# Joints of a streaming-encoder layer: chunk 2's operands copied inside SBUF, sums and splits reordered, a third raw weight buffer in the gates

## The chip, the core and the metric

One core of a Trainium2 chip runs the whole kernel. The time is the device time of one execution in microseconds (us); the figure given for a kernel is the median of its runs. A profile is one execution taken by the hardware profiler. Engines: TensorE (PE, its weight loads PEld), VectorE (DVE), ScalarE (ACT), GpSimd (POOL) and SyncE (SP), which here issues nearly all DMAs, in order.

## The reference

One layer of a chunk-causal encoder over 1024 prompt tokens and 32 sample tokens that share the weights; D = 1024, hidden size of the MLP 4096, fp32 throughout:

```python
h = rms_norm(x, g_mix)
q, k, v, ch, cb, cc, ga, gb = split(h @ w_in)
a = window_attention(q, k, v, sink) @ w_attn_out
u = cc * ch
bo = (cb * causal_conv3(u)) @ w_conv_out
x = x + (sigmoid(ga) * a + sigmoid(gb) * bo) @ w_mix_out
hc = rms_norm(x, g_cross)
x = x + cross_attention(hc @ w_cq, mem_k, mem_v) @ w_co
hm = rms_norm(x, g_mlp)
x = x + square(relu(hm @ w_up)) @ w_down
y = rms_norm(x, g_final)
```

The outputs are y of both groups, and the new keys, values, convolution rows and memory keys and values.

## The kernel before

**Number format.** TensorE works on fp32r operands. Each fp32 operand is split in two: a high half (ACT casts it, L127) and a low half (DVE subtracts the high one, L128; for activations `split_here`, L1255 to L1258). Each product is three matmuls into one accumulator: wh·hi, wh·lo, wl·hi.

**Layout.** Activations lie with features on the 128 partitions (NF = 8 tiles of features) and tokens along the free axis. Up to the cross-attention the 1056 tokens go in chunks of 384, 384 and 288 (`CH`). The last chunk holds the sample. In the MLP they go in two halves of 528 (HT), each of two quarters of 264 (QT).

**Stages, in order of time.**
- Norm, input projection, convolution and window attention (0 to some 550 us), then the attention output.
- The gates. `gate_pair(f)`, f = 1 to 7, computes two column tiles of the gate weights at once with seven half products in place of eight, in Winograd's form. For that it needs sums of weight quarters. POOL makes them earlier: `sum_step` loads a piece (tile `ws` or the shared tile `xacc`), makes four adds and stores it (gsum_d; for the down projection wsum_d).
- Three trunks, one per chunk: eight tiles of w_conv_out and eight of w_mix (`do_mix`) as fillers. `beside` runs one step of the cross-attention of the chunk before after each filler: row statistics (`chunk_stats`), `do_cq`, head units (`scores`, `turn`, `values`) and `do_co`, which adds w_co's product to the residual x1 and has `square_acc` add the squares on POOL.
- `normed(c, f)` (L1243) multiplies x1 by gain and row factor into a temporary (tag "ct", a ring of six) and stores it to DRAM (xn_d, by token halves). For chunk 0 it also splits it in SBUF.
- Up projection of token half 0, w_up's first 16 of 32 tiles paired with the others by `UP`: six weights per quarter in two passes (`up_one`, q = 0 and q = 1, 24 matmuls of 264 columns each), then ten weights for both quarters at once (`up_two`, two items of 24 each). Beside these 32 fillers the cross-attention of chunk 2 and the norm of chunks 1 and 2 are done.
- The sums joint. `comb_load` loads both token halves from xn_d, `comb_sums(k)` makes four combined operands (n3, t2, n1, n4) and splits all four; `up_fetch` and `up_sums` load raw weights and have POOL make their sums; `up_start` begins.
- The paired stage, `up_pair(i)`, i = 0 to 15: the rest of the up projection in the same form, over weight and token halves. It stores hidden activations and their sums to DRAM (op_d, called b_d, n_d and t_d in the rows), which are the operands of the down projection.
- Down projection: stages b11, b21, n4, t2, n3, n1, b22 (`stage`, eight items each by output tile pair j and half t of the 16 operands). After each item `pump2(2)` splits the operands loaded last and loads two of the next stage. Then `final` writes y, chunk by chunk.

**What sets the order.** A planner places the program's operations on the engines; `pin` keeps an instruction at its place in program order. Buffers come from pools of fixed depth. SP's queue is in order, so a DMA that waits for a buffer holds up all that follow it. Weights come through `fetch_w` (raw, tag "wr", two buffers), `issue_w` (split into "wh" and "wl", three buffers each) and `next_w`, which keeps two weights ready beyond the one in use (LOOK = 2). For a weight in `kept` the low half is stored to DRAM (wl_d) at its first use, and loaded at later ones in place of DVE's subtraction.

The accumulators of the stages up to the sums are three buffers (tag "acc"). `lslot` gives one of six tiles of 528 columns (tag "lt"). `put` collects stores, and `flush` issues them at the next item. L854 to L856 are the three matmuls of `product` (gates and up projection), L1640 to L1642 those of the down projection, L216 the column sums of the row statistics, L1310 `up_two`'s copy of an accumulator.

Of the kernel before, what the change touches and what calls it, by code (L numbers as in the profile page):

```python
# [40 lines left out]
def hybrid_step(ctx: ExitStack, tc: tile.TileContext, io):  # L41
# [46 lines left out]

    gsum_d = dram.tile([7, P, 2, 2, 512], F32, name="gsum_d")
# [52 lines left out]
    fetched = []  # L142

    def fetch_w():
        raw = wp.tile([P, 1024], F32, tag="wr", bufs=2, name=nm("wr"))
        src = weight(worder[wpos[0] + len(fetched)])
        sp.dma_start(raw.rearrange("p (i c) -> p i c", i=4) if len(src.shape) == 3 else raw, src)
        fetched.append(raw)
# [536 lines left out]
    pieces += [(j, t, i) for j in range(4) for t in range(2) for i in range(4)]  # L685

# [6 lines left out]
    def sum_step():  # L693
        old = W.pop("new", None)
        if pieces:
            at = pieces.pop(0)
            t = sum_tile(len(pieces))
            if at[0] == "g":
                _, f, q = at
                for e in range(2):  # L700
                    src = io["w_in"][34 + 8 * e + f].rearrange("p (h c) -> p h c", h=2)
                    pin(pool_e.dma_start(t[:, 2 * e : 2 * e + 2], src[:, :, 256 * q : 256 * q + 256]))
            else:
                pin(pool_e.dma_start(t, io["w_down"][at]))
            W["new"] = at, t
        if old:
# [3 lines left out]
            if at[0] == "g":  # L710
                _, f, q = at
                for w in range(2):
                    pin(pool_e.dma_start(gsum_d[f - 1][:, w, :, 256 * q : 256 * q + 256], t[:, 2 * w : 2 * w + 2]))
            else:
                pin(pool_e.dma_start(wsum_d[at], t))
# [152 lines left out]
    def close_gates():  # L868
        pump(0)
        assert not wanted  # L870
        closed(Y["cm"])
        open_top()
        for c in (1, 2):
            wanted.extend((bcp[c], k, bc_d[c][:, k], CH[c][1], lambda c=c: yslot(c)) for k in range(NF))
# [21 lines left out]
    def gate_pair(f):  # L896
# [22 lines left out]
        w1 = take(("w_in", 34 + f))  # L919
        load_a(0)  # L920
# [6 lines left out]
        fetch_w()  # L927
# [71 lines left out]
    def after_gates():  # L999
# [5 lines left out]
        m_cm, mpool = opened("mpool", bufs=16, reuse_waits="tile")  # L1005
# [168 lines left out]
    def do_co(c, half):  # L1174
        def fn(w):
# [3 lines left out]
            for f in fs:  # L1179
# [9 lines left out]
                square_acc(x, f, c)  # L1189
# [14 lines left out]
    def close_cross():  # L1204
        closed(cr_cm)

    def open_sums():
        closed(Y["cm"])
        closed(Y["cm", 1])
        S["s"] = ctx.enter_context(tc.tile_pool(name="sums", bufs=8, reuse_waits="tile"))  # L1210
        L["cm"], L["pool"] = opened("late", bufs=1, reuse_waits="tile")

# [30 lines left out]
    def normed(c, f):  # L1243
        t = tmp(CH[c][1])
        pin(dve.scalar_tensor_tensor(t, x1[c][f], col(G_MLP + f), R[c], op0=ALU.mult, op1=ALU.mult))
        for h, to, at in in_halves(c):
            sp.dma_start(xn_d[h][:, f, to], t[:, at])
# [31 lines left out]
    UP = [(8 * g + i, 8 * g + i + 4) for g in range(4) for i in range(4)]  # L1279

    def up_one(i, q):


        def fn(w):
# [9 lines left out]
            act.activation(h, h, AF.Relu)  # L1294
            pool_e.tensor_tensor(h, h, h, op=ALU.mult)
# [4 lines left out]
    def up_two(i):  # L1300
# [14 lines left out]
        def second():  # L1315
# [6 lines left out]
            pool_e.tensor_tensor(h, h, h, op=ALU.mult)  # L1322
# [7 lines left out]
    def comb_load(kinds):  # L1330
        for kind in kinds:
            for k in range(4):
                h, f = {"t2": (0, k), "n1": (1, k), "n3": (1, k + 4), "n4": (0, k + 4), "b22": (1, k + 4)}[kind]
                pool = S["b" if kind == "b22" else "s"]
                hi, lo = comb[kind, k] = tuple(slot(pool, kind, HT) for _ in range(2))
                sp.dma_start(lo.bitcast(F32), xn_d[h][:, f])

    def raw(kind, k):
        return comb[kind, k][1].bitcast(F32)

    def comb_sums(k):
        both = xacc_tile()
        n3, n1 = both[:, :HT], both[:, HT:]
        t2, n4 = lslot(), lslot()
        pin(dve.tensor_sub(n3, raw("n1", k), raw("n3", k)))
        pin(dve.tensor_sub(t2, raw("t2", k), n3))
        pin(dve.tensor_sub(n1, raw("t2", k), raw("n1", k)))
        pin(pool_e.tensor_tensor(n4, raw("n4", k), t2, op=ALU.subtract))
        for kind, x in (("t2", t2), ("n1", n1), ("n3", n3), ("n4", n4)):
            hi, lo = comb[kind, k]  # L1350
            pin(act.copy(hi, x))
            pin(dve.tensor_sub(lo, x, hi.bitcast(F32)))
# [7 lines left out]
    raws, wset = {}, {}  # L1360

# [56 lines left out]
    def up_pair(i):  # L1418
# [10 lines left out]
        doubled(banks_of(B[i]), wset[i, 3], 0, "n3", False)  # L1429
        h22 = lt()  # L1430
# [21 lines left out]
        m3, m2 = lt(), lt()  # L1452
        dve.tensor_sub(m3, h12, h22)
        put(op_d["n3"][:, i], m3)
        dve.tensor_sub(m2, h11, m3)
        put(op_d["t2"][:, i], m2)
        pool_e.tensor_tensor(h12, h11, h12, op=ALU.subtract)
        put(op_d["n1"][:, i], h12)
# [11 lines left out]
        m4 = h11  # L1470
        pool_e.tensor_tensor(m4, h21, m2, op=ALU.subtract)
        put(op_d["n4"][:, i], m4)
# [40 lines left out]
    def cross_steps(c):  # L1513
        units = [Cross(c, h) for h in ([0, 1, 2, 3] if c < 2 else [4, 0, 1, 2, 3])]
        nu = len(units)
        steps = [("call", [mem_load] if c == 0 else [mem_load_s] if c == 1 else [])]
        steps.append(("call", [lambda: chunk_stats(c)]))
        steps.append(("items", [(do_cq(c, j), ("w_cq", j)) for j in range(2)]))
        for i in range(nu + 2):
# [7 lines left out]
            steps.append(("call", calls))  # L1527
            if i < nu:
                steps.append(("call", []))
        if c == 2:  # L1530
            steps.append(("call", [close_cross]))
        steps.append(("items", [(do_co(c, 0), ("w_co", 0))]))
        steps.append(("items", [(do_co(c, 1), ("w_co", 1))]))
        steps.append(("call", [lambda: chunk_stats(c)]))
# [24 lines left out]
    left = beside([], trunk(0), [(i, lambda: pump(2)) for i in range(NF)])  # L1559
    item(lambda: pump(0))  # L1560
    left = beside(cross_steps(0), trunk(1))
# [8 lines left out]
    late = [(f // 2, lambda f=f: normed(1, f)) for f in range(NF)]  # L1570
    late += [(3 + f // 4, lambda f=f: second_load(f)) for f in range(NF)]
    late += [(4 + f // 4, lambda f=f: second_split(f)) for f in range(NF)]
    steps = left + cross_steps(2)
    at = len(steps)
    late.append((at, open_sums))
    late += [(at + f // 4, lambda f=f: normed(2, f)) for f in range(NF)]
    late.append((at + 1, lambda: comb_load(["t2", "n4"])))
    late.append((at + 2, lambda: comb_load(["n3", "n1"])))
    late += [(at + 4 + 2 * k, lambda k=k: comb_sums(k)) for k in range(4)]
    late.append((at + 4, lambda: up_fetch(0)))  # L1580
    late.append((at + 7, lambda: up_sums(0)))
    late.append((at + 9, lambda: up_fetch(1)))
    assert at + 11 <= len(fillers)
    left = beside(steps, fillers, late)
    assert not left
    worder.append(STOP)

    def up_start():
# [3 lines left out]
        comb_load(["b22"])  # L1592
        up_issue(0, 3)
        up_sums(1)
        up_t2(0)
        comb_split("b22")
# [47 lines left out]
    def banks_for(j, q):  # L1644
        if q is None:
            return banks_of(wide_tile())
        if j % 2 == 0:
            bank["pair"] = wide_tile()
        one = bank["pair"][:, j % 2, :QT]
        return [one, None] if q == 0 else [None, one]  # L1650

    def prod(kind, j, t, then, q=None):


        def fn(w):
            if t == 0:
                bank[j] = banks_for(j, q)
# [198 lines left out]
```

## Time and profile before

| | |
|---|---|
| median of 3 runs | 1796.79 us (1793.31 to 1799.98) |
| the profiled execution | 1801.2 us, span 1799.4 us |
| mean granted clock of TensorE | 0.984 |
| PE busy | 1743.8 us, 97% of the span |
| DVE, ACT, POOL busy | 66%, 47%, 33% |
| DMA | 346.79 MB, mean 193 GB/s; HBM 251.97 MB read, 92.68 MB written |
| share of 16 DMA engines | hardware queue q1 49.8%, software queue q0 7.8% |
| chain that ended last | PE 85%, DMA 6%, DVE 4% |

The span is that of the instructions; the profiled time has 1.8 us more around it. A row of a group reads: line, engine, operation, output<-inputs by the program's names, shape, count, then busy time and mean ns of one, then the idle time before it and what ended most of that. A row of waits reads: the waiting engine and group, the group that released it, the idle time in us, how often, and the longest one. A row of the timeline reads: start, duration, and in brackets the idle time before and its releaser. SPq is SP issuing a DMA.

### The profile page before, as it was taken

Reading aid. Unit: us, or ns where it says so; the run is one execution under the profiler, and the core shown is the slowest. Engines: PE = TensorE matmul, PEld = TensorE weight load, DVE = VectorE, ACT = ScalarE, POOL = GpSimd, SP = SyncE. Lnnn points to the kernel's source line nnn. Section 1 sums busy time; section 2 is a strip of 40 time slices with the busy share of each in tenths; the row PEclk is TensorE's granted clock in tenths of the full one; section 3 lists DMA queues with packets and bytes.
Section 4 is the critical chain, followed back from the end, with each engine's and each line's share of the span. In section 5 each row is a group of like instructions: output and inputs, shape, how many; then the busy total and the mean of one; then the engine's idle time right before and its main releaser. Section 6 shows DMA issues by size and latency. Waiting matters only on the chain.

```text
span 1799.4 us, 32416 instructions
## 1 busy us (share of the span) xinstructions
PE 1743.8 (97%) x12214; PEld 1722.0 (96%) x12214; DVE 1185.3 (66%) x2215; ACT 851.1 (47%) x1648; POOL 596.9 (33%) x659
## 2 busy tenths in 40 slices
PE   8999999999999999999999989979999999999997
PEld 8999999999999999998999988979999999999997
DVE  7776767868666747446675867686666676556664
ACT  8643535435344334334565756554444443433443
POOL 0013245653453444402224241445565400000021
PEclk9999999999999999999999989989999999999999
DMA  5332234344347887868756767565676675555554
GB/s 182 110 101 92 87 113 145 122 147 142 127 151 245 300 291 258 281 205 267 258 198 199 236 222 225 202 232 185 224 230 220 219 262 175 188 181 185 181 177 144
DMA packets 181084, 346.79 MB, mean 193 GB/s; under 512 B 18480, under 2 KB 101712, under 8 KB 180800
## 3 DMA queue, kind: packets, MB, share of 16 engines
q1 hardware_dynamic: 167152, 296.32, 49.8%
q0 software_dynamic: 13776, 48.41, 7.8%
q8 instruction: 96, 1.57, 0.4%
q14 instruction: 60, 0.49, 0.1%
HBM read 251.97 MB, written 92.68 MB: 192 GB/s over the span
## 4 chain that ended last, share of the span: by engine, by line
PE 85%; DMA 6%; DVE 4%; issue 2%; ACT 1%; SPq 1%; POOL 0%; DVEq 0%; ACTq 0%; POOLq 0%
PE acc L185 12%; PE acc L187 12%; PE acc L186 12%; PE acc L1640 6%; PE acc L1642 6%; PE acc L1641 6%; PE acc L854 5%; PE acc L856 5%; PE acc L855 5%; PE pc L856 2%; PE pc L855 2%; PE pc L854 2%; PE pt L574 2%; DVE wl L128 1%; DMA wr<-in_w_up 1%
## 5 line engine op out<-in xcount | busy, mean ns | idle before, releaser
L127 ACT CAST wh<-wr 128x1024 fp32r<-128x1024 f32 x223 | 234.1, 1050 | 440.6 <-PE acc L1641 142.0
L128 DVE TENSOR_TENSOR wl<-wr,wh 128x1024 fp32r<-128x1024 f32 x223 | 287.9, 1291 | 144.3 <-ACT wh L127 143.3
L185 PE MATMUL acc<-X,wh 128*128 128x384 f32 (+1 forms) x864 | 282.1, 327 | 7.0 <-ACT wh L127 7.0
L186 PE MATMUL acc<-X,wh 128*128 128x384 f32 (+1 forms) x864 | 279.3, 323 | 0.0
L187 PE MATMUL acc<-X,wl 128*128 128x384 f32 (+1 forms) x864 | 278.7, 323 | 0.3 <-DVE wl L128 0.3
L261 POOL TENSOR_TENSOR xacc<-xacc,ct 128x384 f32<-128x384 f32 (+1 forms) x62 | 79.9, 1293 | 332.9 <-ACT ct L259 331.0
L185 PEld LDWEIGHTS acc<-X,wh 128*128 128x128 f32 x864 | 163.1, 189 | 7.6 <-ACT wh L127 7.0
L186 PEld LDWEIGHTS acc<-X,wh 128*128 128x128 f32 x864 | 163.4, 189 | 0.6
L187 PEld LDWEIGHTS acc<-X,wl 128*128 128x128 f32 x864 | 163.1, 189 | 0.9 <-DVE wl L128 0.8
L185 PE MATMUL acc<-Y,wh 128*128 128x384 f32 (+1 forms) x432 | 138.8, 323 | 0.7 <-ACT Y L764 0.7
L186 PE MATMUL acc<-Y,wh 128*128 128x384 f32 (+1 forms) x432 | 139.3, 323 | 0.1
L187 PE MATMUL acc<-Y,wl 128*128 128x384 f32 (+1 forms) x432 | 139.3, 323 | 0.0
L1641 PE MATMUL acc<-n,wh 128*128 128x264 f32 x352 | 101.9, 289 | 2.2 <-DVE n L1258 2.2
L1640 PE MATMUL acc<-n,wh 128*128 128x264 f32 x352 | 101.4, 288 | 0.0
L1642 PE MATMUL acc<-n,wl 128*128 128x264 f32 x352 | 101.2, 288 | 0.0
L127 ACT CAST PTh<-pt 128x512 fp32r<-128x512 f32 (+3 forms) x94 | 45.8, 517 | 109.5 <-PE pt L574 108.7
L709 POOL TENSOR_TENSOR ws<-ws 128x256 f32<-128x256 f32 x92 | 81.6, 887 | 7.1 <-DMA ws<-in_w_down 1.9
L709 POOL TENSOR_TENSOR xacc<-xacc 128x256 f32<-128x256 f32 x92 | 82.1, 892 | 4.9
L185 PEld LDWEIGHTS acc<-Y,wh 128*128 128x128 f32 x432 | 80.9, 188 | 1.1 <-ACT Y L764 1.1
L186 PEld LDWEIGHTS acc<-Y,wh 128*128 128x128 f32 x432 | 81.1, 188 | 0.4 <-DVE Y L765 0.4
L187 PEld LDWEIGHTS acc<-Y,wl 128*128 128x128 f32 x432 | 81.1, 188 | 0.0
L560 ACT ACTIVATE S<-S,nmx 128x257 f32<-128x257 f32 (+1 forms) x132 | 64.2, 488 | 18.7 <-DVE nmx L555 17.3
(398 smaller groups left out, 5557.8 us busy)
## 6 DMA issues: line engine op xcount, KB each, us to landing
wr<-in_w_up SPq DMA_DIRECT2D x54, 512.0 KB, 4.2
wr<-in_w_in SPq DMA_DIRECT2D x53, 512.0 KB, 3.8
wr<-wsum_d SPq DMA_DIRECT2D x40, 512.0 KB, 3.6
wr<-in_w_conv_out SPq DMA_DIRECT2D x24, 512.0 KB, 4.3
wr<-in_w_mix SPq DMA_DIRECT2D x24, 512.0 KB, 4.3
wr<-in_w_down SPq DMA_DIRECT2D x24, 512.0 KB, 3.7
wl<-wl_d SPq DMA_DIRECT2D x20, 512.0 KB, 4.1
n_d<-Z SPq DMA_DIRECT2D x32, 264.0 KB, 4.5
```

The costliest lines, as they stand in the source:

```text
L127: act.copy(hi, src)
L128: dve.tensor_sub(lo, src, hi.bitcast(F32))
L185: pe.matmul(out, wh[:, a], hi, start=(k == 0), stop=False)
L186: pe.matmul(out, wh[:, a], lo, start=False, stop=False)
L187: pe.matmul(out, wl[:, a], hi, start=False, stop=(k == len(acts) - 1))
L709: pin(pool_e.tensor_tensor(t[:, to], t[:, x], t[:, y], op=ALU.add))
L854: pe.matmul(acc, wh[:, a], hi, start=(start and k == 0), stop=False, skip_group_check=True)
L855: pe.matmul(acc, wh[:, a], lo, start=False, stop=False, skip_group_check=True)
L856: pe.matmul(acc, wl[:, a], hi, start=False, stop=(k == 3), skip_group_check=True)
L1640: pe.matmul(a, wh[:, s], hi, start=(t == 0 and k == 0), stop=False, skip_group_check=True)
L1641: pe.matmul(a, wh[:, s], lo, start=False, stop=False, skip_group_check=True)
L1642: pe.matmul(a, wl[:, s], hi, start=False, stop=(t == 1 and k == 7), skip_group_check=True)
```

## The change

1. Gates: a third raw weight buffer (`wr3`), taken in turn by every third fetch from f = 1 to f = 7, with one fetch more at the start and none in the last pair.
2. `sum_step` gets four more pieces, the weight sums of the first two up pairs (usum_d). `up_ready` loads them, so `up_sums` is no longer called for pairs 0 and 1; `up_second` loads the one raw weight that is needed.
3. The mix pool has 18 buffers instead of 16, and the first conv output of chunk 1 stands between the conv outputs and the mix of chunk 0. The operand pool of chunk 1 is reopened above the others in `close_gates`.
4. `normed` of chunk 0 runs from filler 2 of the third trunk, formerly from 6. The cross-attention of chunk 2, the norms and the sums are put between the 32 up fillers by a table, `then(i, …)`, in place of `beside`'s one step per filler. Column and row part of the statistics stand apart there.
5. `do_co` for c > 0, f > 4 keeps squares as tiles of their own; the column sum on PE takes them one by one.
6. The low halves of the six weights of `up_one` are `kept`. Squared ReLU: one DVE instruction in `up_one`; in `up_two` ACT squares after its ReLU. POOL's multiplication goes in both.
7. `open_sums` comes before `do_co` of chunk 2 and loads the tokens of chunks 0 and 1 from xn_d into the operand buffers (16 DMAs). `normed` of chunk 2 copies its tile from SBUF into the buffers of n1 and n3, beside the store of features 4 to 7. `comb_sums` uses a single sums tile, casts and splits t2 alone, and returns n3, n1 and n4 raw into their buffers by DMA; they are split in `comb_split` later, b22 and n4 inside `up_pair(0)`.
8. The last pair's sums n3, t2, n1, n4 are made within stage b11, after item (1, 0). Stage b11 goes through two output tiles per half t (`paired`). Each j gets an accumulator of its own in the last stage too. `pump2(3)` in place of `pump2(2)`.

```diff
     def fetch_w():
-        raw = wp.tile([P, 1024], F32, tag="wr", bufs=2, name=nm("wr"))
+        if third:
+            third["n"] += 1
+        if third and third["n"] % 3 == 0:
+            raw = third["pool"].tile([P, 1024], F32, tag="wr3", name=nm("wr3"))
+        else:
+            raw = wp.tile([P, 1024], F32, tag="wr", bufs=2, name=nm("wr"))
...
+    pieces += [("u", i, q) for i in range(2) for q in range(2)]
...
         w1 = take(("w_in", 34 + f))
+        if f == 1:
+            third.update(n=2, pool=Y["top"])
+            fetch_w()
+        if f == NF - 1:
+            third.clear()
...
-        fetch_w()
+        if f < NF - 1:
+            fetch_w()
...
-                square_acc(x, f, c)
+                if c and f > 4:
+                    sq = tmp(n)
+                    act.activation(sq, x, AF.Square)
+                    accs[c].append(sq)
+                else:
+                    square_acc(x, f, c)
...
+        for kind in ("t2", "n1", "n3", "n4"):
+            for k in range(4):
+                comb[kind, k] = tuple(slot(S["s"], kind, HT) for _ in range(2))
+        n = CH[1][0] + CH[1][1] - HT
+        for k in range(4):
+            sp.dma_start(raw("t2", k), xn_d[0][:, k])
+            sp.dma_start(raw("n1", k)[:, :n], xn_d[1][:, k, :n])
+            sp.dma_start(raw("n3", k)[:, :n], xn_d[1][:, k + 4, :n])
+            sp.dma_start(raw("n4", k), xn_d[0][:, k + 4])
...
-            sp.dma_start(xn_d[h][:, f, to], t[:, at])
+            if c < 2 or f > 3:
+                sp.dma_start(xn_d[h][:, f, to], t[:, at])
+        if c == 2:
+            sp.dma_start(raw("n1" if f < 4 else "n3", f % 4)[:, HT - CH[c][1] :], t)
...
-            act.activation(h, h, AF.Relu)
-            pool_e.tensor_tensor(h, h, h, op=ALU.mult)
+            dve.scalar_tensor_tensor(h, h, 0.0, h, op0=ALU.max, op1=ALU.mult)
...
-        both = xacc_tile()
-        n3, n1 = both[:, :HT], both[:, HT:]
-        t2, n4 = lslot(), lslot()
+        n3, n1 = xacc[0][:, :HT], xacc[0][:, HT:]
+        t2 = L["pool"].tile([P, 1024], F32, tag="wr2", bufs=2, name=nm("t2"))[:, :HT]
         pin(dve.tensor_sub(n3, raw("n1", k), raw("n3", k)))
+        sp.dma_start(raw("n3", k), n3)
         pin(dve.tensor_sub(t2, raw("t2", k), n3))
         pin(dve.tensor_sub(n1, raw("t2", k), raw("n1", k)))
-        pin(pool_e.tensor_tensor(n4, raw("n4", k), t2, op=ALU.subtract))
-        for kind, x in (("t2", t2), ("n1", n1), ("n3", n3), ("n4", n4)):
-            hi, lo = comb[kind, k]
-            pin(act.copy(hi, x))
-            pin(dve.tensor_sub(lo, x, hi.bitcast(F32)))
+        sp.dma_start(raw("n1", k), n1)
+        hi, lo = comb["t2", k]
+        pin(act.copy(hi, t2))
+        pin(dve.tensor_sub(lo, t2, hi.bitcast(F32)))
+        pin(pool_e.tensor_tensor(t2, raw("n4", k), t2, op=ALU.subtract))
+        sp.dma_start(raw("n4", k), t2)
...
+        if i == 0:
+            comb_split("b22")
+            comb_split("n4")
...
+        if last:
+            behind.append(lambda: [more(sums()), flush()])
+        else:
+            more(m2)
...
+    trunks = [trunk(c) for c in range(3)]
+    trunks[0].insert(NF, trunks[1].pop(0))
...
-    left = beside(left + cross_steps(1), trunk(2), normeds(0, 6))
+    left = beside(left + cross_steps(1), trunks[2], normeds(0, 2))
...
+    kept.update((("w_up", UP[i][0]), None) for i in range(NQ))
...
+    then(16, call(open_sums))
+    then(17, lambda: item(do_co(2, 0), ("w_co", 0)))
+    then(18, lambda: item(do_co(2, 1), ("w_co", 1)))
+    then(19, call(open_late), call(chunk_col, 2))
+    then(20, call(chunk_row, 2))
+    then(21, call(xacc_tile))
+    for f in (0, 4, 1, 5, 2, 6, 3, 7):
+        then(21, call(normed, 2, f))
+    for k in range(4):
+        then(23 + k, call(comb_sums, k))
+    then(27, call(up_second, 0))
+    then(28, call(comb_split, "n1"))
...
-        if j % 2 == 0:
-            bank["pair"] = wide_tile()
-        one = bank["pair"][:, j % 2, :QT]
-        return [one, None] if q == 0 else [None, one]
+        banks = banks_of(wide_tile())
+        return banks if q is None else [banks[0], None] if q == 0 else [None, banks[1]]
...
+    paired = [(j + i, t) for j in (0, 2) for t in range(2) for i in range(2)]
...
-        for n, (j, t) in enumerate(steps):
+        for n, (j, t) in enumerate(paired if kind == "b11" else steps):
             def fn(ws, j=j, t=t):
                 prod(kind, j, t, then, q)(ws)
-                pump2(2)
+                pump2(3)
+                if behind and (j, t) == (1, 0):
+                    behind.pop()()
```

More of the change, by code (lines that the diff above doesn't have):

```diff
@@ L86, in hybrid_step @@
     wsum_d = dram.tile([4, 2, 4, P, 4, 256], F32, name="wsum_d")
+    UP = [(8 * g + i, 8 * g + i + 4) for g in range(4) for i in range(4)]
+    usum_d = dram.tile([2, P, 2, 2, 512], F32, name="usum_d")
     gsum_d = dram.tile([7, P, 2, 2, 512], F32, name="gsum_d")
@@ L871, in close_gates @@
         closed(Y["cm"])
+        closed(Y["cm", 1])
         open_top()
+        Y["cm", 1], Y[1] = opened("ypool1", bufs=16, reuse_waits="tile", side="right")
         for c in (1, 2):
```

149 lines of the change are left out of this document (86 added, 63 removed).

## The prediction

> **What bounds the kernel now.** I read the page first, then the busy time by stretches, then who made TensorE wait, then the chain of waits and the timeline around each of those places.
>
> ```profile
> span 1799.4 us, 32416 instructions
> PE 1743.8 (97%) x12214; PEld 1722.0 (96%) x12214; DVE 1185.3 (66%) x2215; ACT 851.1 (47%) x1648; POOL 596.9 (33%) x659
> ```
>
> TensorE is busy 97% of the span, and the changed program gives it the same matmuls, but for 18 of one column. So only what is lost beside that work can be won. The stretches show it: window, busy time (and count) of PE, PEld, DVE, ACT, POOL, then granted clock, DMA share and GB/s.
>
> ```profile
> 600.00:675.00 75.00, 75.00 (x472) 74.99 (x471) 41.89 (x59) 24.04 (x47) 34.04 (x42) 1.00 0.86 290
> 675.00:700.00 25.00, 22.07 (x119) 20.98 (x118) 18.02 (x26) 11.84 (x20) 12.02 (x14) 0.93 0.81 267
> 825.00:875.00 50.00, 46.61 (x262) 45.02 (x261) 33.96 (x53) 26.82 (x47) 10.68 (x9) 1.00 0.79 269
> 1025.00:1060.00 35.00, 29.82 (x170) 27.32 (x169) 26.11 (x42) 17.38 (x33) 18.17 (x17) 0.85 0.65 220
> 1040.00:1125.00 85.00, 77.15 (x540) 75.18 (x541) 58.80 (x113) 50.95 (x117) 27.20 (x27) 0.90 0.69 219
> 1060.00:1120.00 60.00, 52.87 (x387) 51.22 (x387) 40.43 (x79) 36.65 (x83) 12.53 (x14) 0.91 0.73 225
> 1160.00:1225.00 65.00, 51.24 (x365) 49.18 (x364) 50.88 (x55) 28.12 (x52) 31.02 (x21) 0.89 0.58 200
> 1225.00:1430.00 205.00, 205.00 (x1684) 205.00 (x1683) 134.53 (x168) 94.20 (x127) 116.02 (x80) 1.00 0.68 220
> 1430.00:1480.00 50.00, 47.78 (x362) 46.85 (x362) 39.36 (x68) 28.13 (x45) 5.98 (x4) 0.93 0.74 260
> 1725.00:1750.00 25.00, 22.69 (x158) 21.77 (x157) 14.90 (x23) 9.88 (x15) 5.02 (x4) 0.86 0.39 128
> ```
>
> A stall costs twice: the idle time, and then matmuls at half clock, which the mean clock shows. Loss of a stretch = (window − PE busy) + (1 − clock) × window:
> - 675:700, gates: 2.9 + 1.8 = 4.7 us
> - 825:875, first mix: 3.4 + 0 = 3.4
> - 1025:1060, end of the third trunk: 5.2 + 5.2 = 10.4
> - 1060:1120, up projection of the first quarters: 7.1 + 5.4 = 12.5
> - 1160:1225, sums before the paired stage: 13.8 + 7.2 = 20.9
> - 1430:1480, up to down: 2.2 + 3.5 = 5.7
> - 1725:1750, before the last product: 2.3 + 3.5 = 5.8
>
> Together 63.4 us: the ceiling of this change. The paired stage (1225:1430) loses nothing; it gives a 264-column matmul as 205 / 1684 = 0.122 us.
>
> ```profile
> PE acc L854 <- ACT lt L1310: 10.1, 3, 5.6
> PE acc L854 <- ACT wh L127: 5.9, 4, 2.6
> PE pr L233 <- ACT ct L231: 3.4, 1, 3.4
> PE acc L1184 <- DVE Gb L1046: 2.7, 4, 1.1
> PE acc L1641 <- DVE n L1258: 2.2, 2, 1.3
> PE acc L1641 <- DVE b L1258: 1.7, 2, 1.1
> ```
>
> **The change, part by part.**
>
> Gates. The raw weight waits for its buffer, not for the link: DVE splits it late behind 16 operand splits, only then SP can load.
>
> ```profile
> 677.27 1.21 DVE L128 TENSOR_TENSOR wl<-wr,wh 128x1024 fp32r<-128x1024 f32 x1
> 678.51 0.32 SPq L147 DMA_DIRECT2D wr<-gsum_d  x1
> 685.25 1.04 ACT L127 CAST wh<-wr 128x1024 fp32r<-128x1024 f32 x1 [3.69 <-DMA wr<-gsum_d]
> ```
>
> A third raw buffer lets that load go one weight earlier, some 6 us, more than the 3.69 that ACT idled. I leave 0.5 us: gain 4.2 (0 to 4.7). Against it stand four more weight sums on POOL (the first two up pairs, formerly summed in the joint), which queue ahead of the residual adds of the first conv output.
>
> ```profile
> 768.26 0.57 POOL L715 DMA_DIRECT2D wsum_d<-ws  x1 [0.41 <-POOL ws L709]
> 806.10 1.00 POOL L1032 TENSOR_TENSOR ct<-ct,ct 128x384 f32<-128x384 f32 x1 [37.27 <-DMA mkr<-mk_d]
> ```
>
> POOL is free for 37.27 us there; four sums at the 8 to 10 us that one takes late in the gates (adds, store, wait for the buffer) need 32 to 40. So that add comes 0 to 5 us late, behind it ACT's split of the mixer's operand; three weights of 4 us each are already split ahead. I price it at nothing; without that cover, up to 5 us.
>
> First mix. One conv output of the second chunk now stands between the first chunk's conv outputs and its mix: 24 matmuls, some 4 us, while the last operands are split. Gain 2 of 3.4 (0 to 3.4).
>
> End of the third trunk. Here the normed chunk 0 shares the six temporaries and SP with the mix's input:
>
> ```profile
> 1036.60 0.33 SPq L1247 DMA_DIRECT2D xn_d<-ct  x1
> 1036.98 0.42 SPq L1042 DMA_DIRECT2D ct<-in_x  x1
> 1039.94 0.46 DVE L1046 TENSOR_TENSOR Gb<-acc,ct 128x288 f32<-128x288 f32 x1 [2.45 <-DMA ct<-in_x]
> ```
>
> SP waits for DVE's product, the input behind it is late, DVE waits for the input, PE for DVE. The change moves these eight products four fillers forward, out of the stretch, and with them their eight stores on SP. Late next is DVE's add after each 6-matmul tile of w_co, so I keep 5 of 10.4: gain 5.4 (2 to 9). The squares of the last three tiles are not added on POOL; 18 tiny matmuls replace the adds.
>
> ```profile
> 1061.91 0.56 PE pq L216 x6
> ```
>
> At 0.56 / 6 us each they cost 1.7 us of PE.
>
> Up projection of the first quarters. The low halves of six weights are stored in the first pass and loaded in the second, instead of being subtracted again. That frees DVE of six splits and charges it with twelve relu-squares taken from ACT and POOL: about even. It adds 12 transfers of 512 KB, 6.3 MB. The stretch 1040:1125 keeps the link busy 0.69 × 85 = 58.7 us; the rate at a full link is 290 / 0.86 = 337 GB/s, so 6.3 MB are 18.7 us more: 77.4. Without its loss (7.9 idle + 8.5 clock) PE would need 85 − 16.4 = 68.6 us here. So the link becomes the bound, at 77 us, and I take little: gain 2 of 12.5, with −8 (rival 1) and +9 (all) as ends. The Trainium skill (DMA: Bandwidth & Descriptors, Specifications) speaks against these transfers too: it limits a core's HBM traffic to about 358 GB/s. By that they would be 17.6 us, an estimate, and the sum would rise by 1; no stretch here sustains the figure. The stats of chunk 2 no longer stand behind late weights on ACT, which was the 3.4 us wait of pr; SP however still puts 16 short stores and eight reloads ahead of the second pass's weights.
>
> Sums before the paired stage, the largest term:
>
> ```profile
> 1161.25 6.43 SPq L1247 DMA_DIRECT2D xn_d<-ct  x6
> 1170.64 3.17 SPq L1336 DMA_DIRECT2D n<-xn_d  x6
> 1173.99 0.71 DVE L1345 TENSOR_TENSOR xacc<-n,n 128x528 f32<-128x528 f32 x1 [3.83 <-DMA n<-xn_d]
> 1175.47 0.63 ACT L1351 CAST t<-lt 128x528 fp32r<-128x528 f32 x1 [8.67 <-DVE lt L1346]
> wr<-in_w_up SPq DMA_DIRECT2D x25, 512.0 KB, 3.9
> n<-xn_d SPq DMA_DIRECT2D x12, 264.0 KB, 4.1
> xn_d<-ct SPq DMA_DIRECT2D x8, 144.0 KB, 1.8
> L1245 DVE SCALAR_TENSOR_TENSOR ct<-Gb,prm,R 128x288 f32<-128x288 f32 x5 | 4.1, 873 | 0.0
> ```
>
> Chunk 2 goes to DRAM and back before the first sum; ACT's copy of it stands ahead of ACT's copy of the accumulators (L1310), and PE starves. The change puts 16 reloads of the old tokens before co(2), copies chunk 2 straight into the operand buffers, and casts only t2 in each sum; n3, n1, n4 go back by copies and are split later. The reloads add a wait: the first needs PE's last cross values, the other 15 queue behind, at 0.42 us some 7 us, and behind them co's stored low half and the next weight. With 3.9 landing that is 11 us; PE has 60 matmuls of the up projection and 24 of co before it uses that low half, 60 × 0.122 + 24 × 0.13 = 10.4, and then another 24: 13.4. Covered.
>
> The new chain: eight products of 0.87 are 7 us, then n3, a weight split and t2, 0.71 + 1.2 + 0.71: first t2 at 9.6 us after the row statistics. Each of three further sums first waits for the copy that empties the one sums buffer: 1.8 to 4.1 landing, 0.4 issue, three subtractions of 0.71 make 4.3 to 6.6. The copy inside SBUF is in no row; these two are the nearest, and I take the long one, its size. Last t2: 9.6 + 19.8 = 29.4 (22.5 at best). By the changed order PE has 218 matmuls in between, 26.6 us. So PE waits 2.8 us, and about as much again for n1's round trip, with half clock behind: 5.6 + 3.4, rounded up to 10. Gain 11 of 20.9 (5 to 18). The precomputed weight sums take POOL's six adds per weight pair out of the start.
>
> Up to down:
>
> ```profile
> 1446.17 6.25 DMA b<-b_d
> 1454.52 0.59 PE acc L1642
> ```
>
> The last four operands reuse buffers that the last pair's product frees. They land and are split some 10 us after it; PE has 49 matmuls, 6 us. Taking two output tiles per half of the operands puts some 110 matmuls in between, 13.4 us. The last pair's own sums wait behind it. Gain 4.7 of 5.7 (2 to 5.7). Last product:
>
> ```profile
> 1733.92 2.76 DVE L1258 TENSOR_TENSOR b<-b,b 128x528 fp32r<-128x528 f32 x2
> ```
>
> Two loads per item leave these splits to the joint; three are done two items earlier. Gain 3.8 of 5.8 (0 to 5.8).
>
> Sum: 4.2 + 2 + 5.4 − 1.7 + 2 + 11 + 4.7 + 3.8 = 31.4. The profiled execution took 1801.2 us (its span and 1.8 around it), so 1769.8; the median of the runs is 1796.8, 4.4 below, so 1765.
>
> **The rivals.**
> 1. The link binds the up projection. For: 77.4 busy us in 85 at 0.86, the highest share held over 75 us, take 90. The stretch then loses 5 more, instead of gaining 2 and the half of 5.4 that lies in it: 9.7 worse, 1775. By the skill's 358 GB/s: 58.7 + 17.6 at the same share, 1774, an estimate; the trace has not shown that rate held. Against: stores need not land in time.
> 2. The sums chain is only shortened, the wait moves from ACT's copies to PE's first t2 and n1, and the half clock stays, since it falls after idle times of 1 us (1725:1750): joints give a third of the above, 10 us, 1787 (same).
> 3. No change: the waits were shared by the next late thing each time, 1796.
> 4. Slower: each of the twelve uses of a stored weight waits for its transfer, since the low half can only load once PE has left its buffer. Price: 3.9 landing and 1.05 cast, 5 us, ×12 = 59, less the other gains, 29: 1827. It decides from 2.6 us exposed per weight on (31.4 / 12). Against: loads are issued two weights ahead, 5.9 us of PE.
>
> **How the numbers follow.** Forecast 0.62 (1765; own range 1750 to 1780), rival 1 0.16, rival 2 0.08, rival 3 0.05, rival 4 0.09. The range, 1748 to 1791, takes in the bounds at the low end and rivals 1 and 2, and leaves out rival 4, 3 and the lowest tail. 0.5%, about 9 us, is what a measurement can tell: faster 0.78 (forecast, rival 1), same 0.13 (rivals 2 and 3), slower 0.09.
>
> **What would show it.** After the change the same seven stretches, by their work, should lose some 30 us instead of 63; no wait of PE on the accumulator copies of the two-quarter stage over 1 us; no idle PE in the gates. I am wrong if the link's share in the up projection stands above 0.85 with PE waiting for wh, if PE waits over 5 us for t2, or if POOL's adds at the first conv output are late and ACT with them.

## The result and the profile after

The changed kernel takes 1791.05 us (median of 20 runs, 1778.5 to 1797.57), the kernel before on the same chip 1795.55 us: a ratio of 0.9957, 95% interval 0.9937 to 0.9978. By that interval it is faster, but by 4.5 us where 31 were forecast, and the median lies just above the range (1791.0). Seven of its runs lie at 1778.5 to 1782.4 us (mean granted clock 0.991 to 0.992) and ten at 1792.4 to 1797.6 (0.986 to 0.988), so its median says how many fell into each group, and the profiled execution is one of the upper group. That execution took 1793.1 us, 1791.3 of span. The page first, with the chain that ended last:

```profile
span 1791.3 us, 32530 instructions
PE 1735.8 (97%) x12250; PEld 1717.5 (96%) x12250; DVE 1175.1 (66%) x2221; ACT 853.9 (48%) x1646; POOL 580.5 (32%) x655
PE 73%; DMA 13%; POOL 7%; DVE 3%; issue 2%; ACT 1%; SPq 0%; DVEq 0%; ACTq 0%; POOLq 0%
```

The shares of busy time are within a point of those of before. The chain is not: POOL had 0% of it and now has 7%, DMA has 13% in place of 6%. POOL, idle for two thirds of the time, has come onto the path. PE has 36 matmuls more, not 18. The busy time by stretches shows where (PE, PEld, DVE, ACT, POOL, then granted clock, DMA share, GB/s; the first row is the kernel before, the others the changed kernel):

```profile
799.00:875.00 76.00, 72.61 (x411) 71.02 (x410) 49.95 (x77) 38.69 (x69) 15.88 (x13) 1.00 0.83 282
675.00:700.00 25.00, 23.34 (x133) 21.66 (x132) 20.29 (x28) 13.12 (x22) 11.04 (x14) 1.00 0.81 278
799.00:875.00 76.00, 60.37 (x326) 58.01 (x326) 39.42 (x61) 27.62 (x51) 26.63 (x29) 0.91 0.72 247
1020.00:1060.00 40.00, 35.59 (x249) 33.72 (x249) 32.97 (x61) 25.64 (x53) 13.32 (x14) 1.00 0.65 224
1060.00:1125.00 65.00, 56.41 (x401) 54.30 (x400) 38.46 (x87) 34.22 (x74) 5.94 (x5) 0.92 0.86 291
1160.00:1225.00 65.00, 57.21 (x431) 56.07 (x430) 38.47 (x59) 38.00 (x73) 6.36 (x5) 0.92 0.86 307
1430.00:1480.00 50.00, 50.00 (x413) 50.00 (x412) 41.41 (x73) 31.38 (x49) 6.96 (x5) 1.00 0.85 294
```

The stretch of the first trunk (799:875) has become the worst: PE is idle for 15.6 us in it. The waits of PE name the place; the timeline of POOL, ACT and DVE names the cause:

```profile
PE acc L193 <- DVE ct L1049: 15.1, 3, 12.8
PE acc L864 <- ACT Z L1293: 4.4, 2, 3.8
PE acc L864 <- ACT lt L1354: 4.2, 1, 4.2
PE acc L1204 <- DMA wl<-wl_d: 1.7, 1, 1.7
```
```profile
812.33 1.45 POOL L712 DMA_DIRECT2D ws<-in_w_up  x2 [7.36 <-DMA usum_d<-ws]
818.86 3.13 POOL L719 TENSOR_TENSOR ws<-ws 128x256 f32<-128x256 f32 x4
822.40 1.55 POOL L723 DMA_DIRECT2D usum_d<-ws  x2 [0.41 <-POOL ws L719]
823.98 1.00 POOL L1050 TENSOR_TENSOR ct<-ct,ct 128x384 f32<-128x384 f32 x1
826.06 0.51 ACT L129 CAST M<-ct 128x384 fp32r<-128x384 f32 x1 [17.83 <-DMA usum_d<-ws]
826.60 0.56 DVE L130 TENSOR_TENSOR M<-ct,M 128x384 fp32r<-128x384 f32 x1 [17.08 <-ACT M L129]
```

POOL makes the last of the added weight sums until 822, so its first residual add (L1050) comes at 824, where before it came at 806. ACT's cast of the mixer's operand follows at 826, when the last store has landed. DVE's next work is the subtraction behind this cast, and it stands 17.1 us for it. Only then it takes the next conv output out of its accumulator (L1049), and PE, three accumulators later, has stood for 12.8 us.

The first and last matmuls of each stage in the two traces give the whole account (us; the last column is the final version of the experiments):

```
stage                                  before    after  difference   early sums,
                                                                     halves not stored
before the gates                        657.8    658.2     +0.4        657.6
gates                                   143.2    140.8     -2.4        141.0
first trunk, with one conv output        75.8     90.6    +14.8         73.4
second and third trunk                  179.6    170.4     -9.2        171.0
up projection, to the first t2          148.0    150.4     +2.4        146.0
to the fourth pair                       61.0     62.4     +1.5         63.4
pairs, up to down, to the last product  465.7    459.3     -6.4        459.2
last product and end                     68.3     59.1     -9.2         59.5
span                                   1799.4   1791.3     -8.1       1771.1
```

24 matmuls of w_co (4.2 us) passed from the third trunk into the up projection, so the second and third trunk won 5.0, and the two rows behind them 0.3 together.

### The profile page after: what moved, and what is told of

Its sections match the earlier page's. It is cut to its first block, busy times and chain, and to the rows that moved or that the text cites. A ratio compares the mean times of both kernels' runs of the same rounds, so it can differ in the third digit from the quotient of the medians.

```text
span 1791.3 us, 32530 instructions
## 1 busy us (share of the span) xinstructions
PE 1735.8 (97%) x12250; PEld 1717.5 (96%) x12250; DVE 1175.1 (66%) x2221; ACT 853.9 (48%) x1646; POOL 580.5 (32%) x655
## 4 chain that ended last, share of the span: by engine, by line
PE 73%; DMA 13%; POOL 7%; DVE 3%; issue 2%; ACT 1%; SPq 0%; DVEq 0%; ACTq 0%; POOLq 0%
PE acc L193 10%; PE acc L195 10%; PE acc L194 10%; PE acc L1733 6%; PE acc L1732 6%; PE acc L1731 6%; DMA wsum_d<-ws 3%; PE acc L864 3%; PE acc L866 3%; PE acc L865 3%; DMA wsum_d<-xacc 3%; POOL ws L719 3%; POOL xacc L719 3%; PE pc L866 2%; PE pc L865 2%
## 5 line engine op out<-in xcount | busy, mean ns | idle before, releaser
L129 ACT CAST wh<-wr 128x1024 fp32r<-128x1024 f32 x217 | 227.8, 1050 | 415.9 <-PE acc L1732 125.7
L130 DVE TENSOR_TENSOR wl<-wr,wh 128x1024 fp32r<-128x1024 f32 x217 | 283.3, 1306 | 143.3 <-ACT wh L129 142.0
L269 POOL TENSOR_TENSOR xacc<-xacc,ct 128x384 f32<-128x384 f32 (+1 forms) x56 | 74.1, 1328 | 414.2 <-ACT ct L267 404.2
L193 PE MATMUL acc<-Y,wh 128*128 128x384 f32 (+1 forms) x432 | 139.9, 326 | 12.8 <-DVE ct L1049 12.8
L1731 PE MATMUL acc<-n,wh 128*128 128x264 f32 x352 | 100.0, 284 | 0.0
L1732 PE MATMUL acc<-n,wh 128*128 128x264 f32 x352 | 100.0, 284 | 0.0
L719 POOL TENSOR_TENSOR ws<-ws 128x256 f32<-128x256 f32 x100 | 94.2, 942 | 5.7
L719 POOL TENSOR_TENSOR xacc<-xacc 128x256 f32<-128x256 f32 x100 | 86.9, 869 | 5.5
L864 PE MATMUL acc<-n,wh 128*128 128x264 f32 x256 | 72.7, 284 | 1.0 <-DVE Z L1477 1.0
```

The costliest lines, as they stand in the source:

```text
L129: act.copy(hi, src)
L130: dve.tensor_sub(lo, src, hi.bitcast(F32))
L193: pe.matmul(out, wh[:, a], hi, start=(k == 0), stop=False)
L719: pin(pool_e.tensor_tensor(t[:, to], t[:, x], t[:, y], op=ALU.add))
L864: pe.matmul(acc, wh[:, a], hi, start=(start and k == 0), stop=False, skip_group_check=True)
L1731: pe.matmul(a, wh[:, s], hi, start=(t == 0 and k == 0), stop=False, skip_group_check=True)
```

## The experiments

The first four ran together; the kernel before took 1796.58 us beside them.

**The changed kernel again.** No edit.

> The changed kernel once more, unaltered. Its 20 runs lie in two groups, about 1778 to 1787 and 1792 to 1798 us. Theory: the groups differ in how late POOL's last weight-sum pieces are when the first conv outputs of chunk 0 need POOL and the pieces' buffer; a run of the lower group would show PE waiting under 6 us there instead of 12.8 us. Rival: the groups come from elsewhere in the program (the up projection or the down projection), and the wait at the first conv outputs is 11 to 14 us in every run.

It took 1784.15 us (12 runs, 1779.75 to 1797.05, ratio 0.9948, 0.9926 to 0.9971). The profiled execution was one of 1795.8 us and has the wait, 12.3 us. No run near 1780 us was profiled, so it stays open whether the wait is short there.

**Adds on DVE.** Are the adds late because they queue behind the pieces (A), or the cast because of memory (B)?

```diff
-            (dve if f == NF - 1 else pool_e).tensor_tensor(t, t, t1, op=ALU.add)
+            (dve if c == 0 or f == NF - 1 else pool_e).tensor_tensor(t, t, t1, op=ALU.add)
```

> Changed kernel with the eight residual adds of chunk 0's conv outputs on DVE instead of POOL, so that they no longer stand behind the weight-sum pieces in POOL's queue. Theory A, the adds' place in POOL's queue makes the wait: the 12.8 us of PE and the half clock behind it go, 1774 to 1778 us. Theory B, the mixer operand's tile lies in the memory of the pieces' tile, and ACT's cast waits until the last piece's store has landed: the wait stays at 10 us or more, time 1786 to 1794 us.

1790.63 us, ratio 0.9967 (0.9949 to 0.9984). Its waits and ACT's timeline:

```profile
PE acc L193 <- DVE ct L1049: 12.4, 2, 11.3
```
```profile
824.62 0.51 ACT L129 CAST M<-ct 128x384 fp32r<-128x384 f32 x1 [16.29 <-DMA usum_d<-ws]
```

Theory B: the add no longer depends on POOL, and the cast still waits for the store of `ws`. The pool of the mixer's operands is opened where the pool of `ws` was closed; its first tile may only be written once that store has landed.

**Pieces begun earlier.** The same pieces, one beside every host item.

```diff
-        if i % 2 and i > 1 or i > 11:
+        if i > 1:
             extras.append((1, sum_step))
```

> Changed kernel in which the weight-sum pieces begin earlier: one sum step beside every host item from the third on (30 instead of 25 in that stage), so that some five pieces of about 11 us each leave the end of POOL's queue. Theory (POOL's queue of pieces is what is late, by either way A or B): last piece done before 780 us, no wait of PE over 2 us at the first conv outputs, 1772 to 1778 us. Rival (link or SP are late there too, or the pieces only move the delay into the attention stage): 1785 us or more.

1777.06 us (1774.89 to 1782.2), ratio 0.9897 (0.9881 to 0.9912): 7 us below the changed kernel beside it, 14 below the median of its first 20 runs (its own times spread over 19 us). POOL's last piece, and the first trunk's stretch:

```profile
764.21 1.57 POOL L723 DMA_DIRECT2D usum_d<-ws  x2 [0.41 <-POOL ws L719]
```
```profile
799.00:875.00 76.00, 73.26 (x416) 71.79 (x415) 49.85 (x76) 38.04 (x68) 16.67 (x14) 1.00 0.80 269
```

The last store is issued at 764 instead of 822; the wait is gone and nothing took its place. The stage takes 73.3 us, 2.5 less than before: that is what the inserted conv output was forecast to bring (2).

**The pieces alone**, in the kernel before (their sums stored, not used).

```diff
+    pieces += [("u", i, q) for i in range(2) for q in range(2)]
```

> Kernel before with nothing but the four added weight-sum pieces (their sums are stored and not used). Theory: by the mean of 10.5 to 11 us per piece in the gates the queue ends at 768 + 42 = 810 us and its store lands at 814, 7 us after the first cast of the mixer's operand; PE loses 3 to 10 us, 1799 to 1806 us. Rival: at the 8 us per piece of the queue's end it is done at 801 us and costs nothing (1795 to 1797 us); then it needs the third raw buffer's loads to become late.

1804.04 us, ratio 1.0038 (1.0023 to 1.0053). PE waits 10.1 us at the same place, and the cast names the same store:

```profile
PE acc L187 <- DVE ct L1035: 10.6, 2, 10.1
```
```profile
824.41 0.51 ACT L129 CAST M<-ct 128x384 fp32r<-128x384 f32 x1 [14.44 <-DMA usum_d<-ws]
```

The four pieces alone cost 7 us, without the third buffer. The next four kernels start from the early pieces; the kernel before took 1798.8 us beside them, so they are compared by ratio (0.9897 for their base).

**No third raw buffer.**

```diff
-        if f == 1:
-            third.update(n=2, pool=Y["top"])
-            fetch_w()
...
-        if f < NF - 1:
-            fetch_w()
+        fetch_w()
```

> The version with early weight sums (1777.1 us), without the third raw weight buffer in the gates. Theory of the prediction (the raw weight waits for its buffer): the 2.6 us wait of PE at about 684 us returns with its half clock, 2.4 to 4.7 us more: 1779.5 to 1782 us. Rival: with two pieces' loads less beside them the weights land in time anyway: 1777 us.

Ratio 0.9896 (0.9876 to 0.9915; 1781.37 us): no loss that can be measured. Without the buffer the stretch reads:

```profile
675.00:700.00 25.00, 23.07 (x134) 21.84 (x133) 20.43 (x29) 12.86 (x22) 12.29 (x15) 1.00 0.80 282
```

It loses 1.9 us; with the buffer the changed kernel lost 1.7, the kernel before 4.7. The kernel before with the four pieces loses 1.9 as well, with its two buffers. So two buffers alone do not make the 2.6 us wait and the half clock in the profile of before.

**Low halves of the up weights not stored.**

```diff
-    kept.update((("w_up", UP[i][0]), None) for i in range(NQ))
```

> The version with early weight sums (1777.1 us), in which the low halves of the six up weights are subtracted again in the second pass instead of stored and loaded (12 transfers of 512 KB less, six DVE subtractions of 1.2 us more). Theory of the link (first rival of the prediction): the DMA share in 1060 to 1110 us falls from 0.85 to about 0.72 and the waits there (3.9 us for the second quarters, 3.1 us for a weight) shrink: 1770 to 1774 us. Theory of the prediction's sum (about even): 1775 to 1779 us. If DVE is what is short there: 1780 us or more.

Ratio 0.9867 (0.9847 to 0.9886; 1775.0 us). Stretch 1060:1110 with the stored halves (first row, early pieces) and without them:

```profile
1060.00:1110.00 50.00, 41.42 (x295) 40.11 (x295) 28.07 (x72) 25.67 (x64) 0.00 (x0) 0.90 0.85 285
```
```profile
1060.00:1110.00 50.00, 45.28 (x341) 43.59 (x340) 36.69 (x81) 28.77 (x68) 0.00 (x0) 0.97 0.75 233
```

In the same 50 us PE makes 341 matmuls instead of 295. A raw up weight takes this long to land in 1060:1125, first with the stored halves (early pieces; 5.9 us in the changed kernel), then without them:

```profile
wr<-in_w_up SPq DMA_DIRECT2D x11, 512.0 KB, 4.9
```
```profile
wr<-in_w_up SPq DMA_DIRECT2D x11, 512.0 KB, 3.9
```

The whole stage, from the end of the trunks to the first t2, takes 152.8 and 150.7 us in the two kernels with early pieces and stored halves (this section's base and the one without the third buffer), and 146.0 us here; the later kernels without stored halves whose up projection is otherwise unchanged took 147.7, 148.2 and 149.2. The six subtractions fit on DVE; the transfers were the price, as the first rival had it. The ratios alone would not settle it, since their intervals touch.

**Second quarters without the round trip.** Chunk 0's part is loaded at the first filler, chunk 1's copied in SBUF.

```diff
+        if c == 1:
+            sp.dma_start(xa[1][f][1].bitcast(F32)[:, CH[0][1] - QT :], t[:, : HT - CH[0][1]])
...
-        then(4, call(second_load, f))
+        then(0, call(second_load, f))
```

> The version with early weight sums (1777.1 us), in which the second quarters of token half 0 are not reloaded whole from DRAM behind their stores: chunk 0's part is loaded at the first filler, chunk 1's part is copied from the norm's temporary inside SBUF. Theory (the round trip through DRAM behind 16 stores makes PE wait): the 3.9 us wait for the second quarters goes, and its half clock: 1771 to 1774 us. Rival (SP's queue and the link are full in this stretch): the wait moves to the weights of the second pass, 1776 to 1779 us.

Ratio 0.9900 (0.9883 to 0.9916; 1781.1 us): nothing won. The 3.9 us wait for the second quarters falls to 0.8, but another takes its place:

```profile
PE acc L195 <- DMA wl<-wl_d: 9.5, 2, 7.6
```
```profile
1080.01 0.47 SPq L1283 DMA_DIRECT2D Z<-ct  x1
1080.58 0.53 SPq L166 DMA_DIRECT2D wl<-wl_d  x1
```

SP issues 16 stores and the eight copies from 1066.8 on almost in one row, 13.8 us, and only then the low half that w_cq waits for. The copies are 3.8 us of this block.

**Two tiles for the sums.**

```diff
-        n3, n1 = xacc[0][:, :HT], xacc[0][:, HT:]
+        n3, n1 = (lslot(), lslot()) if k % 2 else (xacc[0][:, :HT], xacc[0][:, HT:])
```

> The version with early weight sums (1777.1 us), in which the combined sums alternate between the one sums tile and two temporaries, so that a sum no longer waits until the copies of the sum before it have emptied the tile. Theory (the single tile makes the chain: two waits of 1.3 to 1.9 us in each of the last two sums): the last t2 is split 5 to 7 us earlier, PE's 4.9 us wait for t2 goes with its half clock: 1770 to 1773 us. Rival: the two temporaries are missing to the up projection's items (a ring of six), or PE then waits for n1: 1776 us or more.

Ratio 0.9916 (0.9895 to 0.9936; 1785.51 us): if anything slower, as the rival said. PE now waits longer for ACT's copies of the up projection's accumulators (three waits for L1354 and one for L1343):

```profile
PE acc L864 <- ACT lt L1354: 8.9, 3, 5.3
PE acc L864 <- ACT lt L1343: 3.6, 1, 3.6
```
```profile
1185.43 0.63 ACT L1380 CAST t<-t 128x528 fp32r<-128x528 f32 x1 [6.53 <-DVE t L1376]
```

The rival's reason, missing temporaries, is not shown. The row shows another for the longest of these waits (5.3 us): ACT stands 6.5 us at the cast of a t2 that DVE has not made yet, and the copies stand behind that cast. The theory fails more plainly: the last t2 was split by 1191.4 us, 16 us before PE took its first t2 (1207.46), and PE's last wait before it, 3.0 us, still ended with a copy of an accumulator.

The last four start from the early pieces without stored halves (0.9867); before took 1798.32 us beside them.

**Two operand loads per item.**

```diff
-                pump2(3)
+                pump2(2)
```

> The version with early weight sums and without stored up halves (1775.0 us; last product 59.5 us from its first operand to the end), with two operand loads per item of the down projection instead of three. Theory of the prediction (the splits left to the joint make the 1.7 us of waits and the half clock before the last product): the last product takes 63 to 65 us, the time is 1778 to 1781 us. Rival (the gain there comes from the separate accumulators): 60 us, 1775 us.

Ratio 0.9879 (0.9861 to 0.9898; 1776.74 us), last product 59.5 us as with three. DVE's splits of the last operands lie as late as before:

```profile
1718.30 2.76 DVE L1294 TENSOR_TENSOR b<-b,b 128x528 fp32r<-128x528 f32 x2
1722.12 1.31 DVE L1294 TENSOR_TENSOR b<-b,b 128x528 fp32r<-128x528 f32 x2
```

The last product begins at 1715.5 here and began at 1731.1 in the kernel before, so the first of these rows stands 2.8 us behind its begin in both. PE no longer waits for them: it has an accumulator of its own for the next output tile and multiplies there in the meantime (its first product for that tile, out of a t operand, starts at 1719.9, amid the splits).

**Shared accumulators in the last stage.** `banks_for` as before.

> The version with early weight sums and without stored up halves (1775.0 us; last product 59.5 us), in which two output tiles share one accumulator tile in the last stage, as in the kernel before. Theory: PE's waits for DVE's adds out of the shared accumulator return, 2.3 us in three waits, perhaps with one half-clock interval: last product 61.5 to 64 us, 1777 to 1780 us. Rival: they were only the trace of a late start: 59.5 us, 1775 us.

Ratio 0.9905 (0.9886 to 0.9924; 1781.32 us); last product 63.1 us, 3.6 more:

```profile
PE acc L1730 <- DVE Ga L1714: 2.5, 3, 1.1
```

PE waits for DVE's adds out of the shared accumulator, as in the kernel before (2.3 us in three waits). The kernel before also waited 1.7 us for the split of b; here, with three loads, that wait is gone, and the last product is 5.2 us shorter than the 68.3 before.

**Squares on POOL.** `square_acc` for all eight tiles.

> The version with early weight sums and without stored up halves (1775.0 us), with the squares of all eight tiles added on POOL again, so 36 column sums of one column less on PE. Theory of the prediction (the last adds on POOL stand in the chain to the row factor): PE saves 36 x 0.11 = 4 us of work and loses it again in a wait for POOL's adds: 1774 to 1778 us. Rival (PE has other work there, the adds are covered): 1771 us.

Ratio 0.9883 (0.9861 to 0.9905; 1777.75 us): unclear. Its one profile reached the first t2 5 us sooner after the trunks; the runs do not bear that out.

**One output tile after the other.** `steps` in b11, the last pair's sums at once.

> The version with early weight sums and without stored up halves (1775.0 us; 459.2 us from the fourth pair to the last product), with the last pair's sums made at once and stage b11 in the order of one output tile after the other. Theory of the prediction: the joint up to down loses its 4.7 us again (PE waits for the last four operands): 463 to 465 us for that part, 1779 to 1781 us. Rival (three loads per item alone bring the operands in time): 459 to 460 us, 1775 us.

Ratio 0.9916 (0.9897 to 0.9934; 1783.09 us). The waits of the joint up to down are back, and the stage takes 463.2 us instead of 459.2:

```profile
PE acc L1727 <- DVE n L1294: 2.1, 2, 1.3
```

The best version is the changed kernel with the pieces begun earlier and the six low halves not stored: 1775.0 us, 1.3% below the kernel before.

## Why the prediction was wrong

Between the two profiled executions the span fell by 8.1 us where 31.4 were forecast. Of the 23.3 that are missing, the first trunk has 16.8 (14.8 lost, 2 forecast) and the up projection with the sums behind it 11.0 (0.3 won, 2 + 11 - 1.7 forecast). The gates, the end of the third trunk and the start have 2.6 more, and the two joints of the down projection brought 7.1 more than forecast. The largest failed step is thus the weight sums, the second the up projection with its sums.

**Weight sums in POOL's queue: the step that failed.** The prediction named the cover (37 us of idle POOL), the price per piece (8 to 10 us) and the loss without cover (up to 5 us), and took nothing. The price was too low. It had been read from the last pieces of the queue. A piece is a chain: wait for the last store to land, issue the load, four adds, issue the store. In the changed kernel the pieces' adds that begin at 688.2 and at 813.8 us lie eleven pieces apart: 11.4 us each, so 46 for four, not 32 to 40. The end of the queue moved further, from 768.3 (before) to 822.4, by 54.1 us: the load of the first added piece now stands ahead of the adds that used to end the queue, and they begin at 776.4 instead of 764.7. What ended the cover was named in part only. It was POOL's next add, but also the first write into the memory that the pieces' tile had held, which waits for the last store to land; with the adds on DVE that second path alone keeps the cast at 824.6. And the loss was not a shift of 5 us: PE stood 12.8 us, and the clock was at half from 3 us into this wait to some 4 us behind it. With early pieces the cover holds: the median is 1777, inside the range, and the first trunk gave 2.5 (forecast 2). The whole sum does not stand even so: that kernel is some 19 us below the one before, not 31.

**Up projection: the first rival's mechanism.** The sum took a gain of 2 with the link as the bound; the stretch lost 13.8 us (65 - 56.41, and 0.08 x 65) where it had lost 12.5. The rival had said 17.5. That the transfers cost more than the DVE time they saved is shown by the stage lengths (146.0 to 149.2 us without them, 150.7 and 152.8 with them) and by the landings. Two of the prediction's own signs of being wrong came here and at POOL: the link's share is 0.86 while PE waits 1.8 us for wh, and POOL's adds are late and ACT with them. (The fourth rival counted twelve uses of a stored half; the program loads six.) The rate of the Trainium skill (DMA: Bandwidth & Descriptors, Specifications), about 358 GB/s, was not held over these stretches: 291 and 307 GB/s at a share of 0.86. Where the share was full for 9.6 us (1210.4 to 1220.0), the DMAs moved 363 GB/s, close to it.

**Sums before the paired stage: length right, wait misnamed, gain too large.** The last t2 was forecast 29.4 us after the row factor, PE's cover 26.6. In the trace the factor is ready at 1180.2, the last t2 at 1210.1 (29.9 later), and PE runs out of work at 1206.2 (26.0 later). The wait was 4.2 us against 2.8. But the last t2 is not what ended it:

```profile
1206.14 0.63 ACT L1380 CAST t<-t 128x528 fp32r<-128x528 f32 x1 [2.43 <-DVE t L1376]
1207.89 2.23 ACT L1293 CAST n<-n 128x528 fp32r<-128x528 f32 x4
1210.02 0.39 ACT L1354 ACTIVATE lt<-acc 128x264 f32<-128x264 f32 x1
1210.46 0.59 PE L864 MATMUL acc<-t,wh 128*128 128x264 f32 x1 [4.24 <-ACT lt L1354]
```

ACT copies the last accumulator only behind the cast of t2 and four casts of n, until 1210.4, and PE starts then. In the kernel without stored halves PE starts at 1188.95, while the last t2 is still being split (1188.92 to 1189.63), and with two tiles for the sums the last t2 was 16 us early and the wait stayed. So the close agreement of the chain is in part luck: PE waited for an accumulator copy, the wait that the prediction expected to stay under 1 us. What an earlier copy would have left of the wait is open.

The fixed window 1160:1225 gained 7.9 (20.9 - 13.0) against 11, but it no longer holds the same work. By the stage lengths the up projection and the sums together won 0.3 of 11.3, and 3.8 without the stored halves. Of the rest, 1.7 us is PE waiting for w_co's stored low half, which the 16 reloads ahead of it delay; that was forecast as covered.

**Column sums.** 18 per chunk and two chunks, so 36: 36 x 0.67 / 6 = 4.0 us by the rows of six, not 1.7. Whether POOL would have been dearer is not settled.

**Gates.** 2.4 came where 4.2 was forecast, and the buffer is not shown to have brought any of it.

**End of the third trunk.** Forecast 5.4, measured 5.0 for the second and third trunk together, by the stage lengths; PE has no wait over 1.4 us left there.

**Up to down.** Forecast 4.7; the part with the pairs gained 6.4, and putting the old order back took 4.0.

**Last product: right sign, one cause left out.** Forecast 3.8 from three loads per item; 9.2 came. The separate accumulators, which the prediction did not price, are worth 3.6 beside three loads, and with them two loads do as well, since PE goes on with the next tile during the late splits. The kernel with three loads and shared accumulators still won 5.2. Two loads with shared accumulators were not run in the changed kernel, so what three loads bring there is not shown.

So the forecast mechanisms of the first mix and of the joint up to down held, and the size of the trunk's end came. The median moved by 4.5 us because an added task on an idle engine ran past its cover (14 us to the kernel with early pieces), because transfers were put on a link that was the next bound, and because at the sums PE still waits for ACT's copies.

## What to carry to other kernels

An engine that is busy a third of the time can still be late: price an added task on it by the whole chain of one piece (store landing, load, work, store), from the mean over many pieces, and ask what is queued behind the last one, the memory of its buffers included. Before trusting a forecast wait that came out in size, look at which row ended it. Where PE waits for operands at a joint, an accumulator for the next output tile can hide late splits, since PE goes on there. Storing a value to save an engine that has time to spare costs the link, and shows up as later landings of everything else.

## What the runs showed of the hardware that was not expected

The same four POOL adds of a piece took from 3.13 us (818.86, above) to 5.28 us (776.43 in the same trace). The half clock began some 3 us into the 12.8 us wait and was over some 4 us behind its end, which came at 828.7 (the outer rows show PE, clock, DMA share and GB/s alone):

```profile
815.90:819.00 3.10, 0.02 (x1) 1.00 0.11 40
819.00:833.00 14.00, 4.23 (x13) 3.75 (x14) 4.97 (x9) 4.45 (x8) 7.07 (x8) 0.51 0.64 222
833.00:836.00 3.00, 3.00 (x19) 1.00 0.88 329
```

PE worked for only 4.2 us of the middle window, so most of the half clock fell into the wait itself. Adding idle time and half clock, as the prediction did for its stretches, counts that part twice: 22.4 us for 799:875, where the stage lost 18.2 (14.8 more than before, and 3.4 that it lost before).
